# Macaron block on one core: product order, engine of the sums and norms, and split width in the two down projections

## The chip, the cores and the metric

The kernel runs on one core of a Trainium2 chip. The metric is the device time of one execution in microseconds; lower is better. TensorE (PE) multiplies matrices, VectorE (DVE), ScalarE (ACT) and GpSimd (POOL) work on rows of 128 partitions, and SyncE (SP) issues most of the transfers between the chip's memory and the on-chip buffers.

## The reference

One block of an encoder on a sequence of 1024 tokens of width 1024, in float32: a feed-forward part, a token mixer and a second feed-forward part, each followed by a layer norm over the residual.

```python
x = layer_norm(DN_ALPHA * x + 0.5 * swiglu(x, ffn1_w_gate[l], ffn1_w_up[l], ffn1_w_down[l]), ln1_g[l], ln1_b[l])
z = x @ w_in[l]
...                       # forgetting attention (8 heads) and RG-LRU (512 channels) on z
mix = jnp.concatenate([fox, lru], axis=-1) @ w_out[l]
x = layer_norm(DN_ALPHA * x + mix, ln2_g[l], ln2_b[l])
x = layer_norm(DN_ALPHA * x + 0.5 * swiglu(x, ffn2_w_gate[l], ffn2_w_up[l], ffn2_w_down[l]), ln3_g[l], ln3_b[l])
```

`swiglu` is `(silu(x @ w_gate) * (x @ w_up)) @ w_down` with an inner width of 4096. The change touches its last factor, the down projection, in both feed-forward parts (FFN1 and FFN2 below), and the layer norms.

## The kernel before

Every large matrix product is done in three matmuls of a shorter float type (`mm3`): each operand is split into a high part, made by a cast on ACT, and a low part, the difference, made on DVE; then high times high (L153), high times low (L154) and low times high (L155) are added up in a PSUM bank.

`down_ffn` (called once for FFN1 and once for FFN2) computes 0.5 * h @ W_down. It splits the output into four quarters, two halves of the tokens by two halves of the columns, and W_down into the blocks 11, 12, 21 and 22, and needs seven products instead of eight. The table `PRODUCTS` says for each which stored combination of h it reads (`h_d[q][idx]`), which block or sum of two blocks stands on the right, and into which quarters (m, j) the result is added with which sign; m is the half of the tokens, j the half of the columns:

```python
1: (4, ("11", "22", ALU.add), ((0, 0, 1), (1, 1, 1))),
2: (5, ("11", None, None), ((1, 0, 1), (1, 1, -1))),
3: (0, ("12", "22", ALU.subtract), ((0, 1, 1), (1, 1, 1))),
4: (3, ("21", "11", ALU.subtract), ((0, 0, 1), (1, 0, 1))),
5: (6, ("22", None, None), ((0, 0, -1), (0, 1, 1))),
6: (1, ("11", "12", ALU.add), ((1, 1, 1),)),
7: (2, ("21", "22", ALU.add), ((0, 0, 1),)),
```

The call gives the order of the products, 5 2 1 4 7 3 6 before. A product loops over 16 f-tiles of the inner width, and in each over four token tiles t of 128 rows; each (f-tile, t) is one `mm3`, so a product has 192 matmuls and the projection 1344. For every f-tile `operands` makes the right operand and the two splits: if the product has a sum, one operation (L476) adds two W_down blocks into a tile `t`, on DVE in the first six products and on POOL in the last; `parts` makes the high part (L465, ACT) and the low part (L466, DVE) of the h tile (x) and of the W_down block or sum (y). High and low part of one f-tile share one tile `ws` of a ring, of 8 in FFN1 and of 10 in FFN2. Blocks of h (`raw`) and of W_down (`wd`) come four f-tiles at a time (`load`, issued by SP, two groups ahead, first `raw`, then the blocks that aren't there yet).

The results of a product lie in PSUM banks, `a` and `s` in turn. During the next product, `add` (L485, DVE) adds them to the rows of the residual, `row` in the trace, which `open_acc` loads and `scale_acc` multiplies by ALPHA (L109, POOL). When both quarters of a token tile are complete, its `layer_norm` runs: statistics in two halves of the columns (L190, DVE), their aggregate (L193), the first multiply (L194), a square root on ACT, four one-column steps (L196 to L199), and then, for all rows but one, a scale on ACT (L201) and an addition on POOL (L202), for the last row one DVE operation (L204). A first-half row is complete when products 5, 1, 4, 7 and 3 are done, a second-half row when 1, 2, 3, 4 and 6 are.

Where the norms run is set by `hooks`, a table from (place of the product, f-tile) to work. In FFN1 the four first-half rows are normed in the last product, and each is transposed on PE (L239) and split into `xT` (L174 on ACT, L175 on DVE) for the mixer's input projection, which follows. In FFN2 they are normed and stored in the last product too. The last `tail` f-tiles of FFN2's last product (5; none in FFN1) run tile by tile: all their f-tiles for token tile 0, then its adds, norm and store, then tile 1, and so on.

The order of instructions on each engine is set by a scheduler at build time from the order of the program and the waits; each engine then runs its own list in order.

## Time and profile before

| what | us |
|---|---|
| median of 3 runs | 2394.06 |
| lowest and highest of them | 2392.41, 2399.23 |
| the profiled execution, whole | 2396.48 |
| its span, first to last instruction | 2394.8 |
| PE busy | 2318.7 |
| DVE busy | 1814.8 |
| ACT busy | 993.3 |
| POOL busy | 383.0 |

All rows below are of the one profiled execution. A row of a timeline gives the start and the length of an instruction in microseconds, its engine, its line in the program, what it writes and reads (buffer numbers left out), and in brackets how long the engine stood idle before it and whose end released it. FFN1's down projection runs from 646 to about 969, FFN2's from 2064 to the end.

### The profile page before, as it was taken

To read this page: it belongs to the slowest core of one execution; us is meant where nothing else is said; L and a number is where in the kernel's file an instruction comes from. 1 tells how busy PE (TensorE), PEld (TensorE's weight loads), DVE (VectorE), ACT (ScalarE), POOL (GpSimd) and SP (SyncE) were. 2 spreads that over 40 slices of the span, in tenths; PEclk is the share of its full clock that TensorE was granted. 3 is DMA by queue.
4 is the path that set the end of the run, shared out by engine and by line. 5 is a ranking of instruction groups with operands and counts; after the bars stand their busy time and mean duration, and the time that the engine had idled before them with its cause. 6 is when DMAs were issued, how large, how long until landed. Compare 5 with 4: busy or idle time off the path is not lost.

```text
span 2394.8 us, 29276 instructions
## 1 busy us (share of the span) xinstructions
PE 2318.7 (97%) x10709; PEld 1927.6 (80%) x10709; DVE 1814.8 (76%) x3059; ACT 993.3 (41%) x1748; POOL 383.0 (16%) x461
## 2 busy tenths in 40 slices
PE   7999999999999998999999898999999999999996
PEld 5888888888888886788888777888888888888885
DVE  7877777777667878866667889776777777568879
ACT  5343333333344444544546755333333333344443
POOL 2020000000000006311134542000000000010015
PEclk8999999999999999999999998999999999999998
DMA  3333233332374442333365812332323233555342
GB/s 129 116 96 115 84 118 101 111 106 93 137 257 160 158 159 71 87 105 95 106 185 141 238 53 75 110 115 84 115 89 127 94 105 115 189 213 186 125 145 88
DMA packets 175775, 298.99 MB, mean 125 GB/s; under 512 B 8128, under 2 KB 100608, under 8 KB 175632
## 3 DMA queue, kind: packets, MB, share of 16 engines
q1 hardware_dynamic: 151984, 216.06, 28.2%
q0 software_dynamic: 23648, 81.07, 9.0%
q8 instruction: 85, 1.39, 0.3%
q14 instruction: 58, 0.48, 0.1%
HBM read 214.22 MB, written 82.87 MB: 124 GB/s over the span
## 4 chain that ended last, share of the span: by engine, by line
PE 85%; DVE 8%; issue 3%; DMA 1%; ACT 1%; POOL 1%; SPq 0%; POOLq 0%; DVEq 0%; ACTq 0%
PE b L154 17%; PE b L155 17%; PE b L153 17%; PE s L155 5%; PE s L154 5%; PE s L153 5%; PE a L155 5%; PE a L154 5%; PE a L153 5%; DVE ws L466 2%; DVE row L194 2%; PE a L851 1%; DMA raw<-in_ffn_w_gate_dram 1%; DVE st L190 1%; PE a L835 1%
## 5 line engine op out<-in xcount | busy, mean ns | idle before, releaser
L153 PE MATMUL b<-As,ws 128*128 128x512 f32 x1024 | 400.7, 392 | 8.2 <-ACT As L244 8.2
L154 PE MATMUL b<-As,ws 128*128 128x512 f32 x1024 | 400.7, 391 | 3.8 <-DVE As L245 3.8
L155 PE MATMUL b<-As,ws 128*128 128x512 f32 x1024 | 400.3, 391 | 0.0
L153 PE MATMUL b<-A,ws 128*128 128x512 f32 x768 | 299.7, 390 | 4.3 <-ACT ws L295 4.3
L154 PE MATMUL b<-A,ws 128*128 128x512 f32 x768 | 299.2, 390 | 0.0
L155 PE MATMUL b<-A,ws 128*128 128x512 f32 x768 | 299.0, 389 | 0.0
L295 ACT CAST ws<-t 128x512 fp32r<-128x512 f32 x256 | 159.5, 623 | 331.0 <-PE b L154 304.3
L465 ACT CAST ws<-raw 128x512 fp32r<-128x512 f32 x224 | 139.2, 622 | 314.8 <-PE a L155 141.3
L466 DVE TENSOR_TENSOR ws<-raw,ws 128x512 fp32r<-128x512 f32 x224 | 167.8, 749 | 120.4 <-ACT ws L465 120.2
L153 PEld LDWEIGHTS b<-As,ws 128*128 128x128 f32 x1024 | 193.3, 189 | 48.7 <-ACT As L244 8.6
L154 PEld LDWEIGHTS b<-As,ws 128*128 128x128 f32 x1024 | 193.5, 189 | 45.4 <-DVE As L245 5.2
L155 PEld LDWEIGHTS b<-As,ws 128*128 128x128 f32 x1024 | 193.5, 189 | 40.2
L295 ACT CAST ws<-raw 128x512 fp32r<-128x512 f32 x192 | 119.2, 622 | 252.1 <-PE b L154 244.5
L296 DVE TENSOR_TENSOR ws<-t,ws 128x512 fp32r<-128x512 f32 x256 | 177.9, 695 | 53.2 <-ACT ws L295 53.1
L154 PE MATMUL a<-ws,ws 128*128 128x512 f32 x512 | 202.0, 395 | 7.0 <-DVE ws L466 6.9
L153 PE MATMUL a<-ws,ws 128*128 128x512 f32 x512 | 201.4, 394 | 1.4 <-ACT ws L465 1.3
L155 PE MATMUL a<-ws,ws 128*128 128x512 f32 x512 | 201.5, 394 | 0.0
L153 PEld LDWEIGHTS b<-A,ws 128*128 128x128 f32 x768 | 144.3, 188 | 34.3 <-ACT ws L295 4.7
L296 DVE TENSOR_TENSOR ws<-raw,ws 128x512 fp32r<-128x512 f32 x192 | 136.9, 714 | 44.7 <-ACT ws L295 44.6
L429 POOL DMA_DIRECT2D h_d<-row x32 | 18.6, 581 | 937.7 <-DVE row L421 906.2
L155 PEld LDWEIGHTS b<-A,ws 128*128 128x128 f32 x768 | 144.3, 188 | 29.9
L154 PEld LDWEIGHTS b<-A,ws 128*128 128x128 f32 x768 | 144.3, 188 | 29.7
(224 smaller groups left out, 4688.7 us busy)
## 6 DMA issues: line engine op xcount, KB each, us to landing
raw<-h_d SPq DMA_DIRECT2D x56, 1024.0 KB, 5.5
h_d<-row POOLq DMA_DIRECT2D x96, 512.0 KB, 3.4
raw<-in_ffn_w_gate_dram SPq DMA_DIRECT2D x32, 1024.0 KB, 5.5
raw<-in_ffn_w_up_dram SPq DMA_DIRECT2D x32, 1024.0 KB, 5.5
wd<-in_ffn_w_down_dram SPq DMA_DIRECT2D x32, 1024.0 KB, 7.8
h_d<-row POOLq DMA_DIRECT2D x32, 256.0 KB, 4.5
raw<-in_w_in_dram SPq DMA_DIRECT2D x16, 512.0 KB, 5.2
row<-in_x_dram SPq DMA_DIRECT2D x12, 512.0 KB, 7.5
```

Source lines behind the costliest of these rows:

```text
L153: mm(out, ah, bh, start=first, stop=False)
L154: mm(out, ah, bl, start=False, stop=False)
L155: mm(out, al, bh, start=False, stop=last)
L190: v.bn_stats(st[:, j, :], a[:, j * H:(j + 1) * H])
L194: v.scalar_tensor_tensor(a, a, mv[:, 0:1], gb[0], op0=ALU.subtract, op1=ALU.mult)
L295: nc.scalar.copy(hi, src)
L296: v.tensor_tensor(lo, src, f32(hi), ALU.subtract)
L429: return nc.gpsimd.dma_start(d[:, 6], s5)
L465: nc.scalar.copy(hi, src)
L466: self.mark = v.tensor_tensor(lo, src, f32(hi), ALU.subtract)
L835: nc.tensor.transpose(pa[:, (j % 4) * P:(j % 4 + 1) * P], p[:, j * P:(j + 1) * P], self.ident)
L851: mm(pv[:, ps], vt[:, j, :], pts[h, qt][j // 4][l][:, j % 4, ps], start=j == 0 and l == 0, stop=j == last and l == 1)
```

## The change

The products run in the order 5 1 4 7 3 6 2 in both projections, so that the first-half rows are complete after the fifth product; the last product, 2, has no sum, and adds into both column halves of the second-half rows.

POOL gets no work of rows any more: `scale_acc` is an ACT operation, the sums are on DVE in every product, and `layer_norm` ends with one DVE operation in every row, in the attention too.

`operands` works for two f-tiles at once: a cast, a low part and a sum are 1024 columns wide instead of 512, and the high and the low part are a `ws` tile each. The rings stay at 8 and 10; the ring of sums has 2 tiles of double size instead of 3.

The norms of the first half begin in the product in place 5 (f-tile 7 in both) instead of place 6. In FFN1 the first two row tiles are transposed in place 5, from banks of the `a` kind, and the other two in place 6. In FFN2 the third and the fourth norm run in the tail, after its first and second token tile; a key (7, t) of `hooks` stands for that. FFN2's tail is 10 f-tiles instead of 5, and eight of these have their split parts in the buffers of W_down blocks that are no longer wanted (`vp`, `wp`).

```diff
--- before.py
+++ after.py
@@ -106,7 +106,7 @@
             self.scale_acc(i)
 
     def scale_acc(self, i):
-        self.nc.gpsimd.tensor_scalar(self.acc[i], self.acc[i], ALPHA, 1.0, op0=ALU.mult, op1=ALU.mult)
+        self.nc.scalar.activation(self.acc[i], self.acc[i], AF.Copy, scale=ALPHA)
 
     @contextmanager
     def psum(self):
@@ -182,7 +182,7 @@
         self.nc.gpsimd.tensor_scalar(gb[0], gb[0], -1.0, 1.0, op0=ALU.mult, op1=ALU.mult)
         self.gb = gb
 
-    def layer_norm(self, i, last=NT - 1):
+    def layer_norm(self, i):
         nc, v, gb = self.nc, self.nc.vector, self.gb
         a = self.acc[i]
         st = self.small.tile([P, 2, 6], F32, tag="st", name=self.nm("st"))
@@ -197,11 +197,7 @@
         v.reciprocal(y, sd)
         v.scalar_tensor_tensor(w, y, w, y, op0=ALU.mult, op1=ALU.mult)
         v.scalar_tensor_tensor(y, w, 1.5, y, op0=ALU.subtract, op1=ALU.mult)
-        if i != last:
-            nc.scalar.activation(a, a, AF.Copy, scale=y)
-            nc.gpsimd.tensor_tensor(a, a, gb[1], ALU.add)
-        else:
-            v.scalar_tensor_tensor(a, a, y, gb[1], op0=ALU.mult, op1=ALU.add)
+        v.scalar_tensor_tensor(a, a, y, gb[1], op0=ALU.mult, op1=ALU.add)
 
     def project(self, out, w, half, wsl=slice(0, P)):
 
@@ -441,8 +437,8 @@
         nc, v = self.nc, self.nc.vector
         NQ, last = FF // P // 8, len(order) - 1
         wd_v = wd.rearrange("(q two p) d -> two p q d", two=2, p=P)
-        with self.pool("dn_gb") as gp, self.pool("dn_b") as bp, self.pool("dn_t", 3) as tp:
-            homes = {"11": bp, "22": vp, "21": wp, "12": wp}
+        with self.pool("dn_gb") as gp, self.pool("dn_b") as bp, self.pool("dn_t", 2) as tp:
+            places = {"11": bp, "22": vp, "21": wp, "12": wp}
             blocks, raws, banks = {}, {}, {}
             self.fetched = None
 
@@ -455,27 +451,34 @@
                 self.fetch(raws[slot], h_d[q][idx].rearrange("f p t -> p f t"))
                 for name in (b, c):
                     if name and (name, q) not in blocks:
-                        t = blocks[name, q] = homes[name].tile([P, 4, H], F32, tag=f"w{q}", name=self.nm("wd"))
+                        t = blocks[name, q] = places[name].tile([P, 4, H], F32, tag=f"w{q}", name=self.nm("wd"))
                         j = int(name[1]) - 1
                         self.fetch(t, wd_v[int(name[0]) - 1][:, 4 * q:4 * q + 4, j * H:(j + 1) * H])
 
-            def parts(src):
-                t = self.wsp.tile([P, 4 * VW], F32R, tag="ws", name=self.nm("ws"))
-                hi, lo = t[:, 0:H], t[:, H:2 * H]
+            def parts(src, home):
+                if home:
+                    t = home[0].tile([P, 4, H], F32R, tag=home[1], name=self.nm("ws"))
+                    hi, lo = t[:, 0:2, :], t[:, 2:4, :]
+                else:
+                    hi, lo = (self.wsp.tile([P, 4 * VW], F32R, tag="ws", name=self.nm("ws"))[:, 0:2 * H]
+                              .rearrange("p (k c) -> p k c", k=2) for _ in range(2))
                 nc.scalar.copy(hi, src)
                 self.mark = v.tensor_tensor(lo, src, f32(hi), ALU.subtract)
-                return hi, lo
+                return [(hi[:, k, :], lo[:, k, :]) for k in range(2)]
 
             def operands(n, f):
+
                 q, j = divmod(f, 4)
+                k = (f - 4 * NQ + tail) // 2 if n == last else -1
+                homes = [(p, f"w{k}") if 0 <= k < 4 else None for p in (vp, wp)]
                 b, c, op = PRODUCTS[order[n]][1]
-                x = parts(raws[NQ * n + q][:, j, :])
-                y = blocks[b, q][:, j, :]
+                x = parts(raws[NQ * n + q][:, j:j + 2, :], homes[0])
+                y = blocks[b, q][:, j:j + 2, :]
                 if c:
-                    t = tp.tile([P, H], F32, tag="t", name=self.nm("t"))
-                    (nc.gpsimd if n == last else v).tensor_tensor(t, y, blocks[c, q][:, j, :], op)
+                    t = tp.tile([P, 2, H], F32, tag="t", name=self.nm("t"))
+                    v.tensor_tensor(t, y, blocks[c, q][:, j:j + 2, :], op)
                     y = t
-                return x, parts(y)
+                return list(zip(x, parts(y, homes[1])))
 
             def product(n, f, t, x, y):
                 self.mm3(banks[n][t], tuple(p[:, t * P:(t + 1) * P] for p in x), y, f == 0, f == 4 * NQ - 1)
@@ -513,7 +516,9 @@
                     banks[n] = [s[t // 2][:, t % 2, :] for t in range(4)]
                 held = []
                 for f in range(4 * NQ):
-                    held.append((f, *operands(n, f)))
+                    if f % 2 == 0:
+                        two = operands(n, f)
+                    held.append((f, *two[f % 2]))
                     if n < last or f < 4 * NQ - tail:
                         for t in range(4):
                             product(n, f, t, *held[-1][1:])
@@ -530,6 +535,8 @@
                 norm(4 + t)
                 if after:
                     after(4 + t)
+                for g in tasks.get((last + 1, t), []):
+                    g()
 
 
 
@@ -876,7 +883,7 @@
                 i, d = tiles.pop(0)
                 self.down_tile(i, list(zip(mix + [mixes[3]], w_fox)), 1.0, (d,))
                 if d:
-                    self.layer_norm(i, 0)
+                    self.layer_norm(i)
                     normed(i)
 
             for n in range(len(units) + AHEAD + 1):
@@ -960,11 +967,11 @@
 
                 n = [lambda i=i: norm(i) for i in range(4)]
                 return {
-                    (6, 0): [lambda: blk.open_xT(vp, 0)], (6, 4): [n[0]], (6, 6): [n[1]], (6, 7): [xT(0, True)], (6, 8): [n[2]],
-                    (6, 9): [xT(1, True)], (6, 10): [n[3]], (6, 11): [xT(2, True)], (6, 12): [xT(3, True)], (6, 13): [lru_columns],
+                    (5, 0): [lambda: blk.open_xT(vp, 0)], (5, 7): [n[0]], (5, 11): [n[1], xT(0, False)], (5, 15): [xT(1, False)],
+                    (6, 3): [n[2]], (6, 7): [n[3], xT(2, True)], (6, 11): [xT(3, True)], (6, 13): [lru_columns],
                 }
 
-            blk.down_ffn(ffn1_w_down[0], h_d[0], (ln1_g[0], ln1_b[0]), (5, 2, 1, 4, 7, 3, 6), vp, wp, finish, xf, hooks, 0)
+            blk.down_ffn(ffn1_w_down[0], h_d[0], (ln1_g[0], ln1_b[0]), (5, 1, 4, 7, 3, 6, 2), vp, wp, finish, xf, hooks, 0)
             blk.open_xT(wp, 1)
             first.append(blk.columns(w_in[0], Q_OFF, K_OFF))
             blk.hp = left.enter_context(blk.pool("mx", 8))
@@ -996,9 +1003,9 @@
 
         def hooks(norm):
             n = [lambda i=i: (norm(i), store(i)) for i in range(4)]
-            return {(6, 5): [n[0]], (6, 7): [n[1]], (6, 9): [n[2]], (6, 11): [n[3]]}
-
-        blk.down_ffn(ffn2_w_down[0], h_d[1], (ln3_g[0], ln3_b[0]), (5, 2, 1, 4, 7, 3, 6), vp, wp, finish, x2_d, hooks, 5, store)
+            return {(5, 7): [n[0]], (5, 13): [n[1]], (7, 0): [n[2]], (7, 1): [n[3]]}
+
+        blk.down_ffn(ffn2_w_down[0], h_d[1], (ln3_g[0], ln3_b[0]), (5, 1, 4, 7, 3, 6, 2), vp, wp, finish, x2_d, hooks, 10, store)
 
 
 # ---- launch: one core; inputs and outputs as the reference has them ----
```

Line numbers of the changed kernel differ a little: the adds are L488, the sums L479, the last operation of a norm L200.

The scheduler's lists show how this moves the work. On DVE, in FFN1 where the first row of the first half is normed, before (`raw`, `wd` blocks of h and W_down; `ws` split parts; `t` sums; `st`, `ln` statistics; `gb` gain and bias; `row` residual rows):

```order
L466 TENSOR_TENSOR ws_7445<-raw_7259,ws_7445 128x512
L193 BN_AGGR ln_7435<-st_7432 128x2
L466 TENSOR_TENSOR ws_7450<-t_7448,ws_7450 128x512
L194 SCALAR_TENSOR_TENSOR row_5579<-row_5579,ln_7435,gb_6430 128x1024
L196 TENSOR_SCALAR ln_7435<-ln_7435 128x1
L197 RECIPROCAL ln_7435<-ln_7435 128x1
L466 TENSOR_TENSOR ws_7481<-raw_7353,ws_7481 128x512
L198 SCALAR_TENSOR_TENSOR ln_7435<-ln_7435 128x1
L466 TENSOR_TENSOR ws_7486<-t_7484,ws_7486 128x512
L199 SCALAR_TENSOR_TENSOR ln_7435<-ln_7435 128x1
L190 BN_STATS st_7501<-row_5580 128x6
```

and now:

```order
L466 TENSOR_TENSOR ws_6850<-raw_6729,ws_6849 128x1024
L194 SCALAR_TENSOR_TENSOR row_5550<-row_5550,ln_6886,gb_6312 128x1024
L466 TENSOR_TENSOR ws_6856<-t_6853,ws_6855 128x1024
L196 TENSOR_SCALAR ln_6886<-ln_6886 128x1
L197 RECIPROCAL ln_6886<-ln_6886 128x1
L479 TENSOR_TENSOR t_6935<-wd_5610,wd_6515 128x1024
L198 SCALAR_TENSOR_TENSOR ln_6886<-ln_6886 128x1
L193 BN_AGGR ln_6968<-st_6965 128x2
L466 TENSOR_TENSOR ws_6898<-raw_6809,ws_6897 128x1024
L199 SCALAR_TENSOR_TENSOR ln_6886<-ln_6886 128x1
L466 TENSOR_TENSOR ws_6904<-t_6901,ws_6903 128x1024
L200 SCALAR_TENSOR_TENSOR row_5550<-row_5550,ln_6886,gb_6313 128x1024
```

Each L466 is twice as wide, the sums (L479) stand in the list, and the norm's last step (L200) has come in from the two other engines.

On POOL, in FFN1's last product, before:

```order
L476 TENSOR_TENSOR t_7484<-wd_5646,wd_7009 128x512
L202 TENSOR_TENSOR row_5578<-row_5578,gb_6431 128x1024
L476 TENSOR_TENSOR t_7517<-wd_5646,wd_7009 128x512
L476 TENSOR_TENSOR t_7551<-wd_5646,wd_7009 128x512
L476 TENSOR_TENSOR t_7584<-wd_5646,wd_7009 128x512
L202 TENSOR_TENSOR row_5579<-row_5579,gb_6431 128x1024
L476 TENSOR_TENSOR t_7618<-wd_5722,wd_7095 128x512
L202 TENSOR_TENSOR row_5580<-row_5580,gb_6431 128x1024
L476 TENSOR_TENSOR t_7652<-wd_5722,wd_7095 128x512
L109 TENSOR_SCALAR row_5578<-row_5578 128x1024
```

and now, from the preparing of the norm's gain to the mixer's first gates:

```order
L182 TENSOR_SCALAR gb_6312<-gb_6312 128x1024
L599 DMA gate_raw<-in_rg_wa_dram 64x64 x2
L599 DMA gate_raw<-in_rg_wx_dram 64x64 x2
L627 TENSOR_SCALAR g_7602<-g_7602 128x512
L599 DMA gate_raw<-in_rg_wa_dram 64x64 x2
L599 DMA gate_raw<-in_rg_wx_dram 64x64 x2
```

The sums, the norm's additions and the scaling have left POOL; what is left prepares the gain and loads and works on the mixer's gates.

On DVE, at the end of FFN2, for the last token tile, before:

```order
L485 SCALAR_TENSOR_TENSOR row_17946<-a_19633,row_17946 128x512
L190 BN_STATS st_20068<-row_17946 128x6
L193 BN_AGGR ln_20071<-st_20068 128x2
L194 SCALAR_TENSOR_TENSOR row_17946<-row_17946,ln_20071,gb_18799 128x1024
L196 TENSOR_SCALAR ln_20071<-ln_20071 128x1
L197 RECIPROCAL ln_20071<-ln_20071 128x1
L198 SCALAR_TENSOR_TENSOR ln_20071<-ln_20071 128x1
L199 SCALAR_TENSOR_TENSOR ln_20071<-ln_20071 128x1
L204 SCALAR_TENSOR_TENSOR row_17946<-row_17946,ln_20071,gb_18800 128x1024
```

and now, for the last two:

```order
L488 SCALAR_TENSOR_TENSOR row_17602<-a_19103,row_17602 128x512
L194 SCALAR_TENSOR_TENSOR row_17601<-row_17601,ln_19391,gb_18365 128x1024
L196 TENSOR_SCALAR ln_19391<-ln_19391 128x1
L197 RECIPROCAL ln_19391<-ln_19391 128x1
L190 BN_STATS st_19433<-row_17602 128x6
L198 SCALAR_TENSOR_TENSOR ln_19391<-ln_19391 128x1
L190 BN_STATS st_19433<-row_17602 128x6
L199 SCALAR_TENSOR_TENSOR ln_19391<-ln_19391 128x1
L193 BN_AGGR ln_19436<-st_19433 128x2
L200 SCALAR_TENSOR_TENSOR row_17601<-row_17601,ln_19391,gb_18366 128x1024
L194 SCALAR_TENSOR_TENSOR row_17602<-row_17602,ln_19436,gb_18365 128x1024
L196 TENSOR_SCALAR ln_19436<-ln_19436 128x1
```

The steps of two tiles are mixed with one another, and two adds and two statistics stand in the place of one.

## Rows read from the trace of the kernel before

**Rows 1.** The page's busy times: per engine us, share of span, instructions.

```profile
PE 2318.7 (97%) x10709; PEld 1927.6 (80%) x10709; DVE 1814.8 (76%) x3059; ACT 993.3 (41%) x1748; POOL 383.0 (16%) x461
```

**Rows 2.** Stretches of 20 us: PE, PEld, DVE, ACT, POOL busy us, clock, DMA.

```profile
860.00:880.00 20.00, 20.00 (x90) 16.57 (x89) 18.18 (x30) 8.88 (x16) 0.00 (x0) 1.00 0.50 175
...
920.00:940.00 20.00, 14.04 (x65) 11.44 (x63) 20.00 (x32) 8.93 (x17) 14.99 (x7) 0.91 0.17 53
...
2360.00:2380.00 20.00, 15.10 (x54) 11.38 (x55) 18.47 (x31) 6.14 (x10) 7.34 (x4) 0.75 0.20 79
```

**Rows 3.** PE in time: start, duration, instruction, [idle before, who ended it].

```profile
646.48 1.45 PE L153 MATMUL a<-ws,ws 128*128 128x512 f32 x4
...
805.08 0.39 PE L153 MATMUL s<-ws,ws 128*128 128x512 f32 x1
...
814.60 0.39 PE L153 MATMUL s<-ws,ws 128*128 128x512 f32 x1
...
939.10 1.11 PE L239 MATMUL s<-ident,row 128*128 128x128 f32 x4 [5.96 <-DVE ln L196]
...
983.38 1.36 PE L239 MATMUL a<-ident,row 128*128 128x128 f32 x8 [2.36 <-POOL row L202]
...
999.03 0.50 PE L153 MATMUL a<-ua,hi 128*128 128x512 f32 x1 [0.26 <-DVE xT L175]
...
2063.94 0.39 PE L153 MATMUL a<-ws,ws 128*128 128x512 f32 x1
...
2065.49 0.50 PE L154 MATMUL a<-ws,ws 128*128 128x512 f32 x1 [1.16 <-DVE ws L466]
...
2380.23 0.39 PE L155 MATMUL a<-ws,ws 128*128 128x512 f32 x1
```

**Rows 4.** PE's waits, 2055 to 2395 us: total, times, longest.

```profile
PE a L154 <- DVE ws L466: 6.9, 3, 3.6
...
PE a L153 <- ACT ws L465: 1.3, 2, 0.8
```

**Rows 5.** DVE in time in FFN2's tail.

```profile
2370.41 0.69 DVE L485 SCALAR_TENSOR_TENSOR row<-a,row 128x512 f32<-128x512 f32 x1 [1.15 <-PE a L155]
...
2372.11 1.28 DVE L194 SCALAR_TENSOR_TENSOR row<-row,ln,gb 128x1024 f32<-128x1024 f32 x1
...
2373.90 0.68 DVE L485 SCALAR_TENSOR_TENSOR row<-a,row 128x512 f32<-128x512 f32 x1
...
2375.59 3.13 DVE L194 SCALAR_TENSOR_TENSOR row<-row,ln,gb 128x1024 f32<-128x1024 f32 x1
...
2389.87 1.28 DVE L204 SCALAR_TENSOR_TENSOR row<-row,ln,gb 128x1024 f32<-128x1024 f32 x1
```

**Rows 6.** POOL in time in FFN2's tail.

```profile
2375.25 2.39 POOL L202 TENSOR_TENSOR row<-row,gb 128x1024 f32<-128x1024 f32 x1 [8.94 <-ACT row L201]
```

**Rows 7.** DVE in time around FFN1's end.

```profile
967.26 0.69 DVE L485 SCALAR_TENSOR_TENSOR row<-a,row 128x512 f32<-128x512 f32 x1 [1.07 <-PE a L155]
...
981.05 2.29 DVE L199 SCALAR_TENSOR_TENSOR ln<-ln 128x1 f32<-128x1 f32 x1
...
996.57 0.68 DVE L617 TENSOR_TENSOR ue<-u,ua 128x512 fp32r<-128x512 f32 x1
```

**Rows 8.** ACT and DVE in time: one cast of 512 columns, two operations of 1024.

```profile
805.34 0.62 ACT L465 CAST ws<-raw 128x512 fp32r<-128x512 f32 x1 [1.59 <-PE s L155]
...
955.61 1.05 ACT L145 CAST w<-raw 128x1024 fp32r<-128x1024 f32 x1 [2.31 <-PE a L155]
...
956.69 1.23 DVE L146 TENSOR_TENSOR w<-raw,w 128x1024 fp32r<-128x1024 f32 x1 [2.13 <-ACT w L145]
```

**Rows 9.** DVE in time near the attention's end.

```profile
1435.19 2.54 DVE L194 SCALAR_TENSOR_TENSOR row<-row,ln,gb 128x1024 f32<-128x1024 f32 x1
```

**Rows 10.** SP's issue of a W_down block, and DVE's sum that waits for it.

```profile
791.37 0.50 SPq L90 DMA_DIRECT2D wd<-in_ffn_w_down_dram  x1
...
799.43 0.69 DVE L476 TENSOR_TENSOR t<-wd,wd 128x512 f32<-128x512 f32 x1 [0.30 <-DMA wd<-in_ffn_w_down_dram]
```

## The prediction

> **What bounds the kernel now.** I read the page's busy times first: PE is busy for 97% of the span [rows 1], so no more can be won than the places where PE stands still or runs slowly. The windows of 20 us then tell where these are. In the middle of a down projection PE is busy for all 20.00 us, with DVE at 18.18 and POOL at nothing. In FFN1's last product PE falls to 14.04 of 20 while DVE is at 20.00 and POOL at 14.99, and in FFN2's last stretch to 15.10 at a granted clock of 0.75 [rows 2]. So the loss lies in the last products alone, where norms, sums and splits meet on DVE and POOL.
>
> PE in time gives its size. Two matmuls 42 apart start at 805.08 and 814.60, so a matmul takes 0.2267 us when nothing is waited for [rows 3]. A product is 192 matmuls (43.5 us), a down projection 1344 (304.7 us).
>
> FFN1: from the first matmul at 646.48 to the first `a<-ua` of the mixer at 999.03 are 352.5 us [rows 3]. The program has there 1344 matmuls of the projection, 96 of the mixer's input projections and 64 transposes. Transposes cost about half a matmul each (the group of 8 at 983.38 took 1.36 us after its first latency, so 0.12 each, 7.6 us in all), so an unbroken PE needs 326.4 + 7.6 = 334 us: 18.5 us are lost. The longest of the waits are 5.96 on DVE and 2.36 on POOL [rows 3]; the rest are shorter ones and matmuls at the lower clock behind them.
>
> FFN2: from 2063.94 to the end of the last matmul, 2380.23 + 0.39, are 316.7 us, against 304.9: 11.8 lost. Of these 1.16 is the first step's [rows 3], and the waits together are 6.9 + 1.3 [rows 4]; the rest is the lower clock after them. DVE then works on to 2389.87 + 1.28 = 2391.15 [rows 5], 10.5 us behind PE, and the last row's store ends the span 3.65 later.
>
> Why DVE is late is in its own rows. The norm's first multiply (L194) took 1.28 us alone at 2372.11 and 3.13 at 2375.59 [rows 5], where POOL began an L202 of 2.39 us at 2375.25 [rows 6]. A norm statistic of one column, L199, took 2.29 at 981.05 [rows 7]. So DVE stands still while POOL reads and writes full rows. The change takes POOL's work away.
>
> **The change part by part.**
>
> *GpSimd's work.* The sums of product 6 go to DVE, 8 operations of 1.15 (1024 columns wide, as the lo parts [rows 8]) in each FFN, 9.2 us. They lie in the sixth product, beside PE's 43.5 us; the last product is now number 2, which has no sum. `scale_acc` goes to ACT: 24 operations of about 1.05 [rows 8], where ACT is 41% busy [rows 1]. Behind a waiting `scale_acc` stand the casts of the next step; the casts take 2 x 1.05 of a step of 5.44, so the row's transfer may be 1 to 2 us late before PE sees it. I take 0, bound 0 to 2. The final norm operation goes from ACT and POOL to DVE: 1.28 us each [rows 5], 1.2 in a row of operations.
>
> *Splits of two f-tiles.* A step is then 24 matmuls, 5.44 us, and the ring of 8 tiles holds two steps. A cast starts 0.26 after its release (805.34 against the matmul at 805.08) [rows 3, 8]. From release: cast of x 1.05, its lo on DVE, and y's lo behind it, each 1.23 or 1.15 in a row [rows 8]: 0.26 + 1.05 + 0.08 + 1.15 + 1.23 + 0.07 = 3.84. It is wanted after 5.44 + 0.23. The slack is 1.8 us, and DVE with a sum has 3 x 1.15 = 3.45 of work per 5.44. So a burst of up to about 2 us on DVE costs nothing. Bursts above that: eight adds (0.6 each) at the starts of products 2 and 3, and the banks of the transposes; the sixth product of FFN1 is the fullest: 8 x 3.45 for the steps, 4.8 for the eight adds, two norms of 4.1 (below), 2.4 for the transposes' lo parts, 43.0 of 43.5 us. I put 2 us of PE's waits for all of these, bound 0 to 6; in FFN2, whose ring has 10 tiles and which transposes nothing, 0.5. At the projection's start the first y lo is of 1.23 instead of 0.69: 0.55 more, in each FFN.
>
> *Order and norms, FFN1.* The first half is final after the fifth product instead of the sixth, and its four norms come four or more f-tiles apart from the middle of the sixth. A row's transposes follow its norm by four f-tiles, 10.9 us, in which DVE has 4.1 + 6.9 = 11.0 to do: just in time. PE then ends its last product at 646.48 + 304.7 (matmuls) + 3.8 (32 transposes) + 2.5 (11 projection matmuls) + 2.5 (stalls, from above) + 0.2 = 960.2. Before it ended at about 968.9, 1.6 after DVE's first add at 967.26 [rows 7]. From there DVE counts. Before it worked from 967.26 to 997.25 [rows 7], 30.0 us with hardly a gap, of which five operations lengthened as at 981.05 [rows 7] are 7.7 too many: 22.3. Product 2 adds into both halves of the columns of the second rows, so behind PE's end there are 4 adds and 4 statistics more, 0.6 each (4.8), and 3 final multiplies of 1.2 (3.6): 30.7. DVE ends with `ue` at 960.2 - 1.6 + 30.7 = 989.3, and the `ua` matmul starts then, a little later for its bank: 989.9 instead of 999.03. **Gain 9** (5 to 15: the upper end if operations of DVE fall in PE's cover, the lower if the bursts cost 6).
>
> *FFN2's end.* PE ends at 2063.94 + 304.9 + 1.7 (start, 1.16 + 0.55) + 0.5 (bursts) = 2371.1 instead of 2380.6: 9.5. The tail of 10 f-tiles is 4 tiles of 30 matmuls, 27.2 us, and the first tile is ready after 6.8. From then DVE has for each of four tiles two adds, two statistics, L194, the small steps and the final multiply. In rows 5 an add, a statistic and the aggregate take 1.7 from 2370.41 to 2372.11, and from there to the next add at 2373.90 1.8; with a second add and statistic (1.2) and the multiply (1.2) that is 5.9, and 5.3 where two tiles' steps fill each other's gaps; I take 5.5. Two norms of the first half, put into the tail, add 4.1 each (two statistics, L194 and the multiply of 1.2, small steps 0.5 as they fill gaps). 6.8 + 22.0 + 8.2 = 37.0 from the tail's start, 9.8 behind PE's end, against 10.5: 0.7. **Gain 10.2** (7.5 to 12.5).
>
> *Attention.* Three norms there get 1.2 us more on DVE, which bounds that stretch, and lose the lengthening: L194 took 2.54 beside POOL [rows 9], 1.26 too much, three such. 3.6 against 3.7: **0** (-1.5 to 1.5).
>
> Sum: 9 + 10.2 + 0 = 19.2 us. Profiled run 2396.48 - 19.2 = 2377.3; the median of the runs shown is 2.42 lower than that run, 2394.06 - 19.2 = 2374.9, so **2375 us**. With the bounds 11 to 28 us the forecast's own range is 2366 to 2383.
>
> **The rivals.**
>
> *A better FFN1.* PE's own work is a bound of 980.5 plus the stalls, 983, for the `ua` matmul. If the planner's order lets DVE's `ue` run early in PE's cover, the gain in FFN1 is 15.5 and the sum 26: 2368. Against it: `ue` stands behind the last norm in DVE's program. Chance 0.08.
>
> *The W_down loads pace FFN1.* Products 5, 1 and 4 now load W22, W11 and W21 one after the other, product 3 W12, one block a group of four f-tiles, and in 1, 4 and 3 the sum waits for it; before, W11 came in product 2, which has no sum. A block issued at 791.37 let its sum start at 799.43, 8.06 later [rows 10]. The cycle is: load freed by the last lo of a group, 0.5 for the issues, 8.05, a sum of 1.15, a lo of 1.2: 10.9, and a group of four f-tiles lasts 10.9. Each us by which a load is later costs a us in each of up to 12 groups. So it decides from a landing above 8.05; at 9 it takes back 11, leaving 8: 2386. For it: DVE waited for such a load once, 0.30 [rows 10]. Against it: the wait was that short. Chance 0.13.
>
> *Slower: larger operations starve the ring.* In FFN1's 56 steps the chain of 3.84 has 1.8 to spare; where norm operations on DVE stand ahead of a lo (five operations of 0.6 to 1.2 a norm), it becomes longer. It gives back all 19.2 if the average step is 0.34 late, a chain of 6.0 instead of 3.84; at 0.6 late it is 33.6 - 19.2 = 14 us slower, 2408. For it: before, the slack was that of four f-tiles in flight, some 6 us, and DVE has 18.18 of 20 us already in mid-product [rows 2]. Against it: 3.45 of 5.44 is 63%, less than that. Chance 0.07. The Trainium skill ("Perfetto Trace Analysis", section "Optimizing Scalar/DVE Operations") speaks for this rival: "If Scalar/Vector aren't saturated, but are causing bubbles on other engines, breaking up instructions may allow work to be completed sooner", and here they are merged. The same section lets grouping pay where the engine is saturated; the trace has DVE at 20.00 of 20 in the last product and at 18.18 in the middle, so by it the merge would pay at the ends only.
>
> *The waits aren't POOL's.* If DVE's work by itself, and not POOL beside it, is what makes PE wait, the waits stay with the sums and multiplies on DVE: about 2391, no change. Against it: the two L194 above, alike but for POOL. Chance 0.07.
>
> **How the numbers follow.** The forecast has 0.65. About 0.3%, 7.2 us, is what a measurement of this kernel can tell from no change, so faster means below 2386.9. The forecast, the better FFN1 and 0.08 of the loads' 0.13 lie there: 0.81. Same: 0.05 of the loads and 0.07 of the waits that stay: 0.12. Slower: the ring, 0.07. The range takes in the forecast's own, the better FFN1 and most of the loads: 2364 to 2387.
>
> **What would show it.** In the changed profile: L194 at 1.2 to 1.3 in every row, and no POOL operation of full rows in the last products; PE busy 19 or more of 20 us up to about 960 and up to 2371; `ua` near 990; DVE's last multiply ending some 10 us behind PE's last matmul. The forecast is wrong if PE shows a wait at every step of FFN1 (ring), at every second step on sums that waited for a W_down load (loads), or if L194 or L199 stays long with POOL idle.

## The result

The changed kernel takes 2380.2 us (median of 4 runs, 2378.68 to 2383.05), the kernel before 2395.0 beside it: a ratio of 0.9933, with a 95% interval of 0.9920 to 0.9947. That is 14.8 us less; 19.2 were forecast, and 2375 us.

The page's busy times of the changed kernel, as in [rows 1]: POOL has fallen from 383.0 to 248.0 us, DVE from 1814.8 to 1778.9, with 2808 instructions instead of 3059.

```profile
PE 2312.7 (97%) x10709; PEld 1923.6 (81%) x10709; DVE 1778.9 (75%) x2808; ACT 962.8 (40%) x1527; POOL 248.0 (10%) x384
```

Stretches of 20 us of the changed kernel, with the columns of [rows 2]: window, then busy us (and instructions) of PE, PEld, DVE, ACT, POOL, granted clock, DMA share, GB/s.

```profile
860.00:880.00 20.00, 20.00 (x90) 16.57 (x89) 19.53 (x23) 8.84 (x10) 0.00 (x0) 1.00 0.22 76
880.00:900.00 20.00, 20.00 (x94) 16.66 (x93) 19.94 (x33) 9.13 (x12) 0.00 (x0) 1.00 0.31 103
...
920.00:940.00 20.00, 20.00 (x94) 16.45 (x93) 8.89 (x9) 9.64 (x11) 0.00 (x0) 1.00 0.39 106
940.00:960.00 20.00, 20.00 (x92) 16.09 (x91) 11.57 (x17) 6.65 (x9) 2.16 (x4) 1.00 0.42 109
960.00:980.00 20.00, 15.07 (x65) 11.84 (x65) 20.00 (x42) 9.57 (x16) 0.61 (x1) 0.83 0.09 23
...
2340.00:2360.00 20.00, 20.00 (x89) 16.54 (x89) 12.94 (x28) 0.89 (x3) 0.00 (x0) 1.00 0.13 52
```

In the kernel before the last of these stretches was:

```profile
2340.00:2360.00 20.00, 17.85 (x78) 14.17 (x76) 20.00 (x27) 8.22 (x15) 16.02 (x8) 0.99 0.25 101
```

The stretch from 920 to 940, where PE had 14.04 us and DVE 20.00, now has PE at 20.00 and DVE at 8.89. The norms have gone into the product before (880 to 900: DVE 19.94, and PE does not wait). What is left in FFN1 lies behind the last product, from 960 to 980. In FFN2 PE is busy for all of the stretch from 2340 to 2360 too, where it had 17.85 us.

PE in time, changed kernel, the rows that answer to [rows 3]:

```profile
645.76 1.44 PE L153 MATMUL a<-ws,ws 128*128 128x512 f32 x4
...
958.24 0.39 PE L155 MATMUL a<-ws,ws 128*128 128x512 f32 x1
...
970.09 1.33 PE L235 MATMUL a<-ident,row 128*128 128x128 f32 x8 [1.73 <-DVE row L200]
...
974.60 0.80 PE L155 MATMUL s<-xT,w 128*128 128x512 f32 x1 [3.18 <-DVE w L146]
...
990.24 0.47 PE L153 MATMUL a<-ua,hi 128*128 128x512 f32 x1 [1.36 <-ACT row L109]
...
2060.85 0.61 PE L153 MATMUL a<-ws,ws 128*128 128x512 f32 x2
...
2062.93 0.50 PE L154 MATMUL a<-ws,ws 128*128 128x512 f32 x1 [1.46 <-DVE ws L466]
...
2367.03 0.39 PE L155 MATMUL a<-ws,ws 128*128 128x512 f32 x1
```

DVE in time, changed kernel, as in [rows 5, 7]:

```profile
956.63 1.29 DVE L488 SCALAR_TENSOR_TENSOR row<-a,row 128x512 f32<-128x512 f32 x2 [2.53 <-PE a L155]
...
988.79 0.69 DVE L624 TENSOR_TENSOR ue<-u,ua 128x512 fp32r<-128x512 f32 x1 [0.30 <-ACT ua L623]
...
2336.20 1.22 DVE L466 TENSOR_TENSOR ws<-wd,ws 128x1024 fp32r<-128x1024 f32 x1
2347.06 1.29 DVE L488 SCALAR_TENSOR_TENSOR row<-a,row 128x512 f32<-128x512 f32 x2 [9.64 <-PE a L155]
...
2374.99 1.28 DVE L200 SCALAR_TENSOR_TENSOR row<-row,ln,gb 128x1024 f32<-128x1024 f32 x1
```

And the group of the norm's first multiply in the changed kernel (shortest, median and longest in ns):

```profile
L194 DVE SCALAR_TENSOR_TENSOR row<-row,ln,gb x24: 1269/1278/1285, 878.1 to 2373.1; 128x1024 f32<-128x1024 f32 x24
```

None of the 24 is longer than 1.285 us, where one took 3.13 [rows 5]. FFN1's last product ends at 958.63, FFN2's last matmul at 2367.42, and DVE's last operation at 2376.27.

From such rows of each kernel's profiled execution a table of stretches can be made. It separates the effects better than whole times, because the stretch between the `ua` matmul and the first matmul of FFN2's up projection (`b<-A`), which holds the mixer and most of the attention, differs from one execution to the next by several us (431.1 to 439.0) without a part of the change in most of it. The columns are: FFN1's first down matmul to the end of its last (E), from there to the `ua` matmul, both together, then from the first `b<-A` matmul to FFN2's first down matmul, FFN2's first down matmul to its last one's end, and from there to DVE's end. Each row is one execution, so small differences in it are noise: the three kernels that leave FFN1 as the change has it (changed, e2, e7) have sums of 344.5 to 345.2. The ratio is that of all runs, with its interval; one execution of the kernel before, 3891 us at a granted clock of 0.56, is left out of it.

| kernel | FFN1 to E | E to ua | sum | b<-A to FFN2 | FFN2 on PE | DVE behind | ratio |
|---|---|---|---|---|---|---|---|
| before | 322.8 | 29.8 | 352.6 | 630.8 | 316.7 | 10.5 | 1 |
| changed | 312.9 | 31.6 | 344.5 | 635.4 | 306.6 | 8.9 | 0.9933 (0.9920 to 0.9947) |
| e1_norm_end_on_pool | 317.7 | 31.8 | 349.5 | 635.0 | 308.6 | 11.8 | 0.9973 (0.9962 to 0.9984) |
| e2_attention_on_pool | 312.8 | 32.4 | 345.2 | 629.7 | 306.6 | 8.9 | 0.9923 (0.9909 to 0.9938) |
| e3_one_f_tile | 309.8 | 31.5 | 341.3 | 634.9 | 306.2 | 8.9 | 0.9922 (0.9905 to 0.9938) |
| e4_before_without_pool | 315.5 | 26.1 | 341.6 | 635.1 | 306.3 | 13.3 | 0.9936 (0.9922 to 0.9951) |
| e5_three_steps | 309.8 | 31.9 | 341.6 | 631.3 | 306.3 | 6.0 | 0.9895 (0.9877 to 0.9914) |
| e6_tail_in_ffn1 | 310.6 | 25.6 | 336.2 | 629.7 | 306.3 | 6.0 | 0.9883 (0.9865 to 0.9901) |
| e7_tail_of_6 | 312.8 | 32.3 | 345.2 | 634.7 | 306.6 | 16.9 | 0.9972 (0.9962 to 0.9982) |
| e8_order_alone | 318.3 | 32.8 | 351.1 | 629.5 | 306.3 | 12.2 | 0.9971 (0.9960 to 0.9983) |
| e9_projections_after | 310.1 | 33.0 | 343.1 | 633.6 | 306.6 | 8.9 | 0.9925 (0.9909 to 0.9942) |
| e10_scaling_on_pool | 314.4 | 33.0 | 347.4 | 634.9 | 306.6 | 8.9 | 0.9937 (0.9919 to 0.9955) |

For the change it says: 8.1 us won in FFN1, 11.8 in FFN2 with what DVE does behind it (327.2 to 315.4), and 4.6 lost between the attention's end and FFN2's down projection. The rest is small: FFN1 began 0.7 earlier, and the mixer took 1.1 longer, the last store 0.3 longer; together 14.6, the difference of the two spans.

### The profile page after: what moved, and what is told of

Same layout as the page of the kernel before. It is cut to its first block, busy times and chain, and to the rows that moved or that the text cites. A ratio compares the mean times of both kernels' runs of the same rounds, so it can differ in the third digit from the quotient of the medians.

```text
span 2380.2 us, 28555 instructions
## 1 busy us (share of the span) xinstructions
PE 2312.7 (97%) x10709; PEld 1923.6 (81%) x10709; DVE 1778.9 (75%) x2808; ACT 962.8 (40%) x1527; POOL 248.0 (10%) x384
## 4 chain that ended last, share of the span: by engine, by line
PE 90%; DVE 6%; issue 1%; DMA 1%; ACT 1%; POOL 1%; SPq 0%; POOLq 0%; DVEq 0%; ACTq 0%
PE b L154 17%; PE b L155 17%; PE b L153 17%; PE s L155 6%; PE s L154 6%; PE s L153 6%; PE a L155 6%; PE a L154 6%; PE a L153 6%; PE a L858 1%; PE a L842 1%; DVE row L200 1%; DVE row L194 1%; DVE st L190 1%; PE a L729 1%
## 5 line engine op out<-in xcount | busy, mean ns | idle before, releaser
L153 PEld LDWEIGHTS b<-As,ws 128*128 128x128 f32 x1024 | 193.4, 189 | 50.5 <-ACT As L240 10.5
L291 ACT CAST ws<-raw 128x512 fp32r<-128x512 f32 x192 | 119.2, 623 | 256.5 <-PE b L154 248.1
L154 PE MATMUL a<-ws,ws 128*128 128x512 f32 x512 | 199.6, 390 | 2.1 <-DVE ws L466 2.1
L155 PE MATMUL a<-ws,ws 128*128 128x512 f32 x512 | 199.5, 390 | 0.0
L153 PE MATMUL a<-ws,ws 128*128 128x512 f32 x512 | 198.8, 390 | 0.1
L465 ACT CAST ws<-raw 128x1024 fp32r<-128x1024 f32 x112 | 117.4, 1050 | 180.1 <-PE a L154 94.9
L466 DVE TENSOR_TENSOR ws<-raw,ws 128x1024 fp32r<-128x1024 f32 x112 | 136.6, 1221 | 60.9 <-ACT ws L465 60.3
L154 PEld LDWEIGHTS b<-A,ws 128*128 128x128 f32 x768 | 144.5, 188 | 29.8
L292 DVE TENSOR_TENSOR ws<-raw,ws 128x512 fp32r<-128x512 f32 x192 | 133.2, 694 | 45.4 <-ACT ws L291 45.3
L153 PE MATMUL s<-ws,ws 128*128 128x512 f32 x384 | 149.5, 389 | 0.0
```

Of the source, the lines that this page charges most:

```text
L153: mm(out, ah, bh, start=first, stop=False)
L154: mm(out, ah, bl, start=False, stop=False)
L155: mm(out, al, bh, start=False, stop=last)
L291: nc.scalar.copy(hi, src)
L292: v.tensor_tensor(lo, src, f32(hi), ALU.subtract)
L465: nc.scalar.copy(hi, src)
```

## The experiments

**The end of the norms back on POOL (FFNs).**

```diff
-        v.scalar_tensor_tensor(a, a, y, gb[1], op0=ALU.mult, op1=ALU.add)
+        if split_end:
+            nc.scalar.activation(a, a, AF.Copy, scale=y)
+            nc.gpsimd.tensor_tensor(a, a, gb[1], ALU.add)
+        else:
+            v.scalar_tensor_tensor(a, a, y, gb[1], op0=ALU.mult, op1=ALU.add)
```

`split_end` is true in both FFNs for every row but the last.

> The changed kernel (2380.2 us) with one step undone: in both FFNs the norm of every row but the last ends again with a scale on ACT and an addition on POOL instead of one DVE multiply-add; the attention keeps the DVE form. My theory, that DVE stands still while POOL works on full rows: behind PE's end in FFN1 the five lengthened operations come back (7.7 us) and three multiplies of 1.2 go (3.6), 4.1 later; in FFN2 five norms in the tail get 1.85 and lose 1.2 each, 3.3 later: about +7, 2387 us, with L194 of 3 us beside L202 again. The rival, that the new order and the spread norms alone made the gain: within 2 us of 2380.

Measured: 2390.1 us, ratio 0.9973. So 0.4 percentage points of the 0.67 are lost by this one step. By the table 5.0 us go in FFN1 and 5.0 in FFN2 (308.6 + 11.8 against 306.6 + 8.85). DVE and POOL in this kernel's tail, in time:

```profile
2372.51 3.20 DVE L194 SCALAR_TENSOR_TENSOR row<-row,ln,gb 128x1024 f32<-128x1024 f32 x1
```

```profile
2372.29 2.34 POOL L202 TENSOR_TENSOR row<-row,gb 128x1024 f32<-128x1024 f32 x1 [1.28 <-ACT row L201]
```

The multiply of 1.28 us is 3.20 again as soon as the addition runs beside it, in the new order too: more than half of the gain goes with the additions. In FFN1 the place was another than I had put it: 4.8 of the 5.0 lie ahead of E (317.7 against 312.9), where the first-half norms run, and not behind it. There a lengthened step can be followed to PE. POOL, DVE and PE in time:

```profile
901.92 2.40 POOL L202 TENSOR_TENSOR row<-row,gb 128x1024 f32<-128x1024 f32 x1 [3.92 <-ACT row L201]
```

```profile
901.96 2.38 DVE L198 SCALAR_TENSOR_TENSOR ln<-ln 128x1 f32<-128x1 f32 x1
```

```profile
908.06 0.65 PE L154 MATMUL s<-ws,ws 128*128 128x512 f32 x1 [1.86 <-DVE ws L470]
```

The low part for which PE waits 1.86 us stands in DVE's list behind the one-column step, 0.21 us alone, that took 2.38. PE has 2.8 us of such waits up to E, 0.64 in the changed kernel, and its busy time there is 2.6 us longer, at a granted clock of 0.99 instead of 1.00.

**The attention's norms back on ACT and POOL.**

```diff
-                    self.layer_norm(i)
+                    self.layer_norm(i, i != 0)
```

The second argument is `split_end`, as above; the FFNs leave it out.

> The changed kernel with one step undone: the attention's norms, all but that of row 0, end on ACT and POOL as before; the FFNs keep the DVE form. The profiles differ by 5.7 us against the change between the mixer's first ua matmul and FFN2's down projection. If that is the price of the three to seven DVE multiplies there, 4 to 5.7 us come back: about 2375.5. The rival, that it is a difference between two executions and the exchange is even, as I had forecast: 2380 within 1.5.

Measured: 2376.8 us, ratio 0.9923. The stretch from `b<-A` to FFN2 is 629.7 instead of 635.4. PE at the attention's end, in time: first the kernel before, then the changed one, then this one.

```profile
1439.68 6.22 PE L239 MATMUL b<-ident,row 128*128 128x128 f32 x32 [3.66 <-DVE row L204]
...
1471.83 0.95 PE L153 MATMUL b<-As,ws 128*128 128x512 f32 x2 [3.27 <-ACT As L244]
```

```profile
1433.70 6.41 PE L235 MATMUL b<-ident,row 128*128 128x128 f32 x32 [5.35 <-DVE row L200]
...
1467.88 1.22 PE L153 MATMUL b<-As,ws 128*128 128x512 f32 x2 [5.10 <-ACT As L240]
```

```profile
1431.00 5.38 PE L239 MATMUL b<-ident,row 128*128 128x128 f32 x32 [3.64 <-DVE row L204]
...
1462.45 1.22 PE L153 MATMUL b<-As,ws 128*128 128x512 f32 x2 [3.41 <-ACT As L244]
```

Two waits are longer by 1.7 and 1.8 in the changed kernel and go back with the undoing. The first is the last norm, which ends 8.18 us behind the first `b<-A` matmul instead of 6.49. The second can be followed back too: the cast for which PE waits (`As`, ACT) waits for DVE, and between the end of its last norm and the step that releases the cast DVE has 44 operations where the kernel before has 42. The two more are low parts of weights, 0.6 each, which the scheduler has put ahead of it; it is 44 in all kernels with the DVE form and 42 in all others. All kernels agree on it: the seven with the DVE form take 633.6 to 635.4 us in this stretch, the five with the ACT and POOL form 629.5 to 631.3. So the exchange is not even here; it costs 4.6 us, the difference of the two means. The whole times alone, 2376.8 against 2380.2 with overlapping intervals, would not have shown it.

**Splits of one f-tile.**

```diff
-                    if f % 2 == 0:
-                        two = operands(n, f)
-                    held.append((f, *two[f % 2]))
+                    held.append((f, *operands(n, f)))
...
-                x = parts(raws[NQ * n + q][:, j:j + 2, :], homes[0])
+                x = parts(raws[NQ * n + q][:, j, :], homes[0], f)
```

> The changed kernel with casts, low parts and sums of one f-tile (512 columns) again, the ring's tiles holding high and low part of one f-tile, everything else as changed, the tail of 10 too. My theory, that the wide operations cost only the first step's 0.55 us twice and save DVE some 5% of its split time: 2380 within 2. The rival of the prediction that larger operations starve the ring: 2375 or less, since the small ones give PE a longer lead.

Measured: 2376.2 us, ratio 0.9922, between the two expectations. FFN1 is 3.2 us shorter (341.3), FFN2 no different (306.2 + 8.8). So the wide operations don't starve the ring, as in the rival; but they don't pay either. In the changed kernel 11 projection matmuls of the mixer (2.5 us) had been put among the last product's, in this one none; that is taken up below.

**The kernel before, with POOL's work taken away and nothing else.**

```diff
-        self.nc.gpsimd.tensor_scalar(self.acc[i], self.acc[i], ALPHA, 1.0, op0=ALU.mult, op1=ALU.mult)
+        self.nc.scalar.activation(self.acc[i], self.acc[i], AF.Copy, scale=ALPHA)
...
-        if i != last:
+        if False:
...
-                    (nc.gpsimd if n == last else v).tensor_tensor(t, y, blocks[c, q][:, j, :], op)
+                    v.tensor_tensor(t, y, blocks[c, q][:, j, :], op)
```

> The kernel before (2395.0 us) with POOL's row work taken away and nothing else: scale_acc on ACT, the sums of the last product and the end of every norm on DVE; old order, hooks, widths and tail. If POOL beside DVE is all there is to it, most of the gain comes: about 2383. My theory needs the order too: the last product then holds 43.5 us of PE and 55 us of DVE work in FFN1 (19.4 of splits, 9.7 of sums, 16.2 of norms, 4.8 of adds, 4.8 of transposes), so PE waits some 10 us where it lost about 10 before: 2395 within 5.

Measured: 2380.4 us, ratio 0.9936: the whole gain, with the old order. My expectation fell, and the simple one held. Three windows of this kernel, columns as above:

```profile
920.00:940.00 20.00, 20.00 (x97) 16.37 (x96) 20.00 (x39) 9.17 (x18) 0.00 (x0) 1.00 0.17 53
940.00:960.00 20.00, 18.14 (x81) 14.42 (x80) 18.75 (x32) 12.17 (x19) 0.00 (x0) 0.91 0.37 95
...
2340.00:2360.00 20.00, 20.00 (x89) 16.50 (x88) 20.00 (x39) 6.83 (x13) 0.00 (x0) 1.00 0.18 71
```

From 920 to 940 DVE is as full as before, 20.00 of 20 us, and PE is at 20.00 instead of 14.04 [rows 2]. I had taken DVE's surplus of 11.5 us for PE's wait. But the splits for which PE waits stand early enough in DVE's list; the surplus falls on norms, and only FFN1's last stretch ahead of E is longer (315.5, where the 1344 matmuls, 32 transposes and the 9 projections put there need 310.6; the window from 940 to 960 has it). Behind E the old order has four adds and four statistics less, 26.1 us instead of 31.6. In FFN1 the two orders come out even: 341.6 here, 341.3 in the new order with the same width (e3_one_f_tile).

**The order alone, POOL keeping the norms' additions and the scaling.** The last product's sums are gone from POOL with the order, since product 2 has none.

```diff
-                    (6, 0): [lambda: blk.open_xT(vp, 0)], (6, 4): [n[0]], (6, 6): [n[1]], (6, 7): [xT(0, True)], (6, 8): [n[2]],
-                    (6, 9): [xT(1, True)], (6, 10): [n[3]], (6, 11): [xT(2, True)], (6, 12): [xT(3, True)], (6, 13): [lru_columns],
+                    (5, 0): [lambda: blk.open_xT(vp, 0)], (5, 7): [n[0]], (5, 11): [n[1], xT(0, False)], (5, 15): [xT(1, False)],
+                    (6, 3): [n[2]], (6, 7): [n[3], xT(2, True)], (6, 11): [xT(3, True)], (6, 13): [lru_columns],
...
-            return {(6, 5): [n[0]], (6, 7): [n[1]], (6, 9): [n[2]], (6, 11): [n[3]]}
+            return {(5, 7): [n[0]], (5, 13): [n[1]], (6, 1): [n[2]], (6, 3): [n[3]]}
...
-(5, 2, 1, 4, 7, 3, 6)
+(5, 1, 4, 7, 3, 6, 2)
```

> The kernel before (2395 to 2396 us) with the new order of the products and the first half's norms spread over the last two products, POOL keeping the norms' additions and scale_acc; splits of one f-tile, tail of 5. After the run of the kernel before without POOL's work, which made the whole gain with the old order, I expect little of the order by itself: the sums of the last product are gone from POOL, so some lengthening goes, but behind PE's end there are four adds and four statistics more: 2391 within 3. If order and spread were a cause of their own: 2385 or less. If they cost: 2395 or more.

Measured: 2388.9 us, ratio 0.9971, within the expectation. In FFN1 it wins 1.4 us (351.1), little more than the table's noise. PE's waits there, up to the mixer (total, times, longest):

```profile
PE a L153 <- DVE xT L175: 4.5, 1, 4.5
PE a L239 <- POOL row L202: 2.8, 1, 2.8
```

In FFN2 it wins on PE what the change wins: 306.3. So FFN2's 10.4 us on PE go with either remedy, POOL's row work taken away, or its sums gone and its additions spread over two products, and they don't add up; FFN1's go with POOL's work only. A lengthened operation of DVE costs PE nothing by itself: in the last 90 us of FFN2's products five are longer than alone here, by 9.2 us together (before: ten, by 13.7), and PE waits for none of them.

**FFN2's tail of 6 f-tiles instead of 10.**

```diff
-hooks, 10, store)
+hooks, 6, store)
```

> The changed kernel with a tail of 6 f-tiles in FFN2 instead of 10. By the prediction's sum: the first token tile is ready after 4.1 us, DVE has 22.0 + 8.2 us of work from then, the tail is 16.3 us of PE: DVE ends 18 us behind PE instead of 8.8, 9 us slower: 2389. The rival, that DVE's idle time of 9.64 us ahead of the tail takes these up: 2381 or less.

Measured: 2388.7 us, ratio 0.9972. DVE in time, the first add of the tail and the last operation:

```profile
2353.54 1.29 DVE L488 SCALAR_TENSOR_TENSOR row<-a,row 128x512 f32<-128x512 f32 x2 [12.41 <-PE a L155]
...
2381.40 1.28 DVE L200 SCALAR_TENSOR_TENSOR row<-row,ln,gb 128x1024 f32<-128x1024 f32 x1
```

DVE ends 16.9 us behind PE, 18 expected. It stands idle for 12.41 us ahead of the tail and then needs 29.1 for what the program gives it only there. Together with the new order and two norms in the tail, its length is worth 8.1 us (16.95 against 8.85); with the old order a tail of 5 left 13.3 (e4_before_without_pool).

**The scaling back on POOL.**

```diff
-        self.nc.scalar.activation(self.acc[i], self.acc[i], AF.Copy, scale=ALPHA)
+        self.nc.gpsimd.tensor_scalar(self.acc[i], self.acc[i], ALPHA, 1.0, op0=ALU.mult, op1=ALU.mult)
```

> The changed kernel with one step undone: scale_acc, 24 operations, on POOL again. If any POOL work on full rows lengthens what DVE does beside it, the two to four of them behind FFN1's end cost 1 to 2 us there, against 1.4 us that PE waited for such an operation on ACT: 2380 within 1.5. The rival, that a POOL operation with one row to read costs as much as the norms' additions with two: 2 us each for the four, 2385.

Measured: 2383.6 us, ratio 0.9937: no difference that this can tell (the change has 0.9933), though FFN1's stretch was 2.9 us longer in the profiled execution. Beside a scaling of 1.04 us on POOL a one-column step of DVE took 0.75:

```profile
969.65 0.75 DVE L199 SCALAR_TENSOR_TENSOR ln<-ln 128x1 f32<-128x1 f32 x1
```

```profile
969.35 1.04 POOL L109 TENSOR_SCALAR row<-row 128x1024 f32<-128x1024 f32 x1 [11.16 <-PE a L235]
```

So this step of the change is worth between nothing and 3 us. The wait of 1.36 on a scaling in ACT's list, ahead of the `ua` matmul, is gone here, and the stretch from E to `ua` is no shorter for it (33.0).

**The projections behind the last product.**

```diff
-(6, 11): [xT(3, True)], (6, 13): [lru_columns],
+(6, 11): [xT(3, True)], (6, 15): [lru_columns],
```

> The changed kernel (2380.2 us) with the mixer's first weight columns split two f-tiles later (15 instead of 13 of FFN1's last product). In the changed kernel the scheduler put 11 of the mixer's projection matmuls among the last product's; with splits of one f-tile, and here, none: all 96 stand behind it. Theory for why splits of one f-tile were 3 us faster up to the ua matmul: these 11 matmuls, 2.5 us, hold back the last product, and so DVE's chain behind it, while PE waits for that chain later anyway. Then this kernel takes 2.5 us less between FFN1's first matmul and the ua matmul: 342.0 instead of 344.5, 2377.5 in all. The rival, that the width of the operations itself costs: 344.5 and 2380, or more.

Measured: 2381.0 us, ratio 0.9925. FFN1's product ends 2.7 us earlier behind its first matmul (310.1), as it should with 11 matmuls less in front; but behind it 1.3 of that are given back, and the sum is 343.1, where the theory had 342.0 and its rival 344.5. It explains somewhat less than half of what splits of one f-tile won, and 1.4 us in one execution of each is not far above the table's noise of 0.7. Of the rest, 1.8 us, 1.2 lie behind E: the same 129 instructions keep PE busy for 28.27 us here and for 27.07 with splits of one f-tile, at a granted clock of 0.90 and 0.95. What holds the clock lower here stays open.

**Three steps together.** The attention's norms and the splits as in the runs above, and:

```diff
-            return {(5, 7): [n[0]], (5, 13): [n[1]], (7, 0): [n[2]], (7, 1): [n[3]]}
+            return {(5, 7): [n[0]], (5, 13): [n[1]], (6, 1): [n[2]], (6, 3): [n[3]]}
```

> The changed kernel (2380.2 us) with three steps: splits of one f-tile; the attention's norms ending on ACT and POOL except row 0's; FFN2's third and fourth norm in the last product at f-tiles 1 and 3 instead of in the tail, where DVE stood idle for 9.64 us before the tail began. If the three are independent: 2.6 us from the splits, 2.4 from the attention, 3 from the norms, whose two times 4.1 leave the tail so that DVE ends one tile's 5.9 us behind PE instead of 8.8: about 2372. The rival, that the norms' work only takes the place of splits and PE waits for them: 2375, with a wait of PE on ws before FFN2's tail.

Measured: 2371.4 us, ratio 0.9895. As far as one execution can tell the three are independent: 341.6 in FFN1, 631.3 from the attention on, and DVE ends 6.0 behind PE in FFN2 instead of 8.85. DVE in time, the last add and the last multiply of this kernel:

```profile
2359.76 1.29 DVE L495 SCALAR_TENSOR_TENSOR row<-a,row 128x512 f32<-128x512 f32 x2 [0.85 <-PE a L155]
...
2364.42 1.28 DVE L204 SCALAR_TENSOR_TENSOR row<-row,ln,gb 128x1024 f32<-128x1024 f32 x1
```

DVE now waits for PE ahead of the last tile's add, 0.85, and only that tile's steps are left behind PE.

**A tail in FFN1 too.** On top of the three steps:

```diff
-(5, 1, 4, 7, 3, 6, 2), vp, wp, finish, xf, hooks, 0)
+(5, 1, 4, 7, 3, 6, 2), vp, wp, finish, xf, hooks, 6,
+                         lambda k: [(wp, f"w{2 * k + j}") if k < 2 else None for j in range(2)])
```

> The kernel of three steps, and FFN1's last product too ends tile by tile, over 6 f-tiles, four of which have their parts in the W_down buffers wp. Theory: behind PE's end in FFN1 DVE's chain of about 31 us (8 adds, 8 statistics, 4 norms, the mixer's first steps) sets the time; with the tail it begins 12.2 us earlier, and then PE's own 85 projection matmuls and 32 transposes, 23 us, set it: 31.5 becomes 23.5, 8 us faster than the kernel of three steps, about 2364. The rival, that transposes or a low part of the mixer's weights still wait behind the norms in DVE's order: 3 us or less.

Measured: 2367.2 us, ratio 0.9883, the best of all kernels here: 0.5% less than the changed kernel. E to `ua` is 25.6 us, 6.3 shorter than without the tail (8 expected, 3 or less by the rival); FFN1's product is 0.8 longer with it, so 5.4 are left up to `ua` (336.2 against 341.6). PE's waits in it from 640 to 1010 us (total, times, longest):

```profile
PE s L239 <- DVE xT L175: 0.9, 1, 0.9
PE a L153 <- DVE xT L175: 0.3, 1, 0.3
```

The wait of 3.18 on a low part of the mixer's weights, which the changed kernel shows at 974.60, is gone: DVE had held it behind the late norms.

## Why the prediction was right, and where it was not

**The bound.** That the loss lay in the last products and that DVE was slow there because of POOL was right. It is shown from both sides: the kernel before without POOL's rows makes the whole gain (0.9936), and the changed kernel with the additions back on POOL loses more than half of it (0.9973), with L194 of 3.20 us back. So the rival that the waits aren't POOL's is out. That DVE as a whole stands still beside POOL was too broad: some of its operations are held and others never (last section). Two things go with POOL's rows, the lengthening of DVE's operations and the 2.4 us of POOL's own addition, for which PE's transposes waited 2.36 us [rows 3]; these runs don't say how much of the gain is each one's.

**FFN1: 9 forecast, 8.1 measured.** Up to E the step by step sum held: PE's stalls are 1.9 us (312.9 against 311.0 for 1344 matmuls, 32 transposes and 11 projections), 2.5 forecast. E to `ua` is 31.6, 29.7 forecast; DVE's own work was right there (from its first add at 956.63 to the end of `ue` at 989.48 it has 31.0 us and 1.9 idle; 30.7 forecast), but it wasn't the only chain. One term was missing: PE waited 3.18 for a low part of the mixer's weights, which DVE made after most of the late norms, so the mixer's matmuls came late, and DVE stood idle for 1.6 of the 1.9 us until ACT had copied a result of them. PE also waited 1.36 on the scaling that now stands in ACT's list, the wait behind a waiting operation that I had put at 0 with a bound of 2; that it cost time is not shown, since with the scaling on POOL the stretch is no shorter. E came earlier than forecast and the stretch behind it was longer, so that the sum came out this close is in part luck.

The prediction's working has four slips that change little. The product's end before, 968.9, is the start of its last matmul; it ended at 969.26, 2.0 behind DVE's first add and not 1.6. PE's second longest wait in FFN1 before was one of 2.49 us on DVE's `xT` and not the 2.36 on POOL. The upper bounds of the three parts add up to 29 and not 28. The gain of the better FFN1 is 16 by its own figures and not 15.5.

**FFN2: 10.2 forecast, 11.8 measured.** PE 10.1 (9.5 forecast). DVE ends 8.85 behind it (9.8 forecast). The tail's sum from the rows of single operations was right within about a microsecond, and again in the run with a tail of 6, 16.9 against 18.

**Attention: 0 forecast, a loss of 4.6 measured.** This is the term that was mis-sized, and outside its bounds of -1.5 to 1.5. I set three multiplies of 1.2 against three lengthenings of 1.26. Of the L194 there only one was lengthened by that much [rows 9], and one by 0.5; and seven norms there changed their form, not three. I counted only up to the last norm, which came 1.7 late. A second wait, longer by 1.8, comes some 30 us later, at the start of FFN2's up projection, behind the two low parts that DVE now makes first. That it belongs to the norms' form is shown by the undoing, which takes it away; why the scheduler moves the low parts with it is not shown. The two make 3.5 of the 4.6.

**What the order does.** The prediction took the order for a part of the cause, since it lets the first half be normed earlier. The runs say otherwise: in FFN1 the two orders come out even once POOL is idle, because the new one leaves four adds and four statistics more behind E. In FFN2 either remedy wins the same 10 us. What the new order and the longer tail add there is 4.5 us behind PE's end (13.31 to 8.85).

**The rivals.** A starved ring did not come: PE shows no wait by the step, and the windows in mid-product stand at 20.00. The narrow splits were 3.2 us faster in FFN1 all the same, in part by the way the work lies at the end of the product and not by a wait in each step; the one wait that they save in FFN1's products is the first step's, 0.64 at 647.84. So the Trainium skill's sentence on breaking up instructions ("Perfetto Trace Analysis", section "Optimizing Scalar/DVE Operations") agrees with these runs in its direction, by 3.2 us, but beyond that first step not by the bubbles that it names. The W_down loads did not pace FFN1 either: DVE's sums waited for them 7 times, 15.8 us in all where it had been 0.3, but PE waited for no sum behind them. The better FFN1 did not come by itself; a tail in FFN1, on top of the three steps, brings most of it (336.2 against the 334 of an unbroken PE).

**The whole.** 19.2 forecast, 14.8 measured: the sum missed by 4.4. The attention's 4.6 is about that; the other misses, FFN1 short by 0.9, FFN2 over by 1.6 and the 0.7 that the stretches outside the table lost, cancel one another.
